# Scores of the second attention from two float32r parts stacked on the partitions, with the residual kept in DRAM meanwhile

## The chip, the cores and the metric

One NeuronCore of a Trainium2 chip runs the whole program. The metric is device microseconds from start to end of one launch; the time of the kernel before is the median of three runs. Engine names: PE is TensorE, PEld its weight loads, DVE is VectorE, ACT is ScalarE, POOL is GpSimd, SP the engine whose queue issues the DMAs.

## The reference, cut to what matters

The reference is two transformer blocks on x of 256 tokens by 1024 channels, in float32. The first block (indexed attention, pooling branch, a feed-forward layer of 16384 experts) is not touched by the change. The second block begins with a normalised projection to many parts: a recurrent branch (1344 channels), 16 query heads of 64, keys and values of 4 groups in three kinds (compressed, selected, window), gates, and two branch gates. Its attention, for each query head r of group g, is

```python
qh = rms_norm_2(heads(q, 16), q_norm_g)
k_cmp = rms_norm_2(compress(kc), ...); k_slc = rms_norm_2(ks, ...); k_win = rms_norm_2(kw, ...)
o_cmp = softmax(mask_cmp(qh @ k_cmp.T * scale)) @ v_cmp     # 15 compressed keys
o_slc = softmax(causal(qh @ k_slc.T * scale)) @ v_slc       # 256 keys
o_win = softmax(causal(qh @ k_win.T * scale)) @ v_win       # 256 keys
o = g0 * o_cmp + g1 * o_slc + g2 * o_win
```

With 256 tokens every block of keys is selected and the window covers them all, so the selected and the window kind are two plain causal softmaxes over different keys. After it x = x + (gated sum of the branches) @ w_out, then a feed-forward layer with its own residual x = x + ... .

## The kernel before, in words

Activations lie with channels on the partitions (x is [128, 8, 256]: 8 chunks of 128 channels, 256 tokens). Weights come as units of 512 KB: SP loads one into a raw buffer (`load`, L100), ScalarE copies it to a float32r tile `wh` (L164), VectorE or GpSimd subtracts to get the remainder `wl` (L165). `weights` (L169) hands the units out in a fixed order and keeps some ready ahead. `mm3` (L181) multiplies a unit with an activation that is split in the same way, in three float32r products: high by high, high by low, low by high; 24 matmuls of 256 columns for one unit.

The order in which each engine executes is laid down when the kernel is built. It follows the program's text with other work drawn forward where the dependencies allow it: a memset of the keys' tile (L956) stands between updates of x (L888), and transposes of one attention step stand between the scores of another. Each engine executes its own queue in order, except that weight loads can run ahead of matmuls.

The second block, in the program's order:

- L887 to L899: x is updated for the last time in the first block (L888, one VectorE operation per chunk), split by `make_xg` (L264), multiplied with the first three weight units; `sum_sq` and `rms_finish` give the token scale `r3` (reciprocal at L262).
- `proj` (L918) makes one projection of 128 channels into PSUM. Eleven go to the recurrent branch (L1026 to L1030), four to the inputs of the compression (L1035 to L1062; its tile `cb` shares the tag `P`), one to the gates, four to the values.
- `recur` (L1066) is the scan of the recurrent branch, advanced in pieces between projections.
- The keys, L1119 to L1133: for two kinds and two chunks c, the projection is scaled (`zs`, L930), squared, summed over each 64 channels by a float32 matmul with `blk64` (`hs` at L940, in `head_scale`), and VectorE writes the normalised keys (L1126). One chunk holds two groups, one on partitions 0 to 63 and one on 64 to 127. ScalarE copies each half to the other half as well (L1129), because a head's query lies on one half of the partitions. `ks` holds 15 compressed keys, one zero column and 256 selected keys, `kw` 256 window keys. The compressed keys are added at L1147.
- The queries, L1136 to L1156: eight projections, one ScalarE copy each with the norm's weight (L1154). One query chunk holds two heads, on 64 partitions each. Their norms are collected by `head_sq` and enter as a scale of the exponential.
- `nsa` (L1181) is a generator: for each group g and each block b of 128 queries there are five steps: scores of two heads and their exponentials, scores of the other two, then normalisation (L1247 to L1253) and the transposes of the compressed part, then twice transposes and products with the values. In block 0 two heads share one score tile; in block 1 each head has one of two PSUM banks. There are two score tiles. Scores are float32 matmuls with 64 rows (L1194, L1196, L1220, L1226), each in two records of the profile; masks are added by bf16 products of an identity with `mk0` and `mk1` (L1199, L1222, L1224, L1228). VectorE takes maxima (L1201, L1204, L1230, L1231), ScalarE makes exponentials with sums.
- L1313 to L1323: 26 more projections (recurrent gate and branch gates), with one or two steps of `nsa` after each. Then `wup2` (19 blocks for each of 8 output chunks), `wout2`, whose result is added to x (L1375), the feed-forward layer, and the last addition to x with the store of the output (L1411, L1412).

x stays in its tile in SBUF from the start to the end.

Of the kernel before, what the change touches and what calls it, by code (L numbers as in the profile page):

```python
# [7 lines left out]
F32 = mybir.dt.float32  # L8
# [50 lines left out]
def tile_kernel(ctx: ExitStack, tc: tile.TileContext, I, out):  # L59
    nc = tc.nc  # L60
# [14 lines left out]
    x = const.tile([128, 8, 256], F32, name="x")  # L75
# [8 lines left out]

    ones = const.tile([128, 128], F32, name="ones")
# [162 lines left out]
    def sum_sq(wpool_, tot, k, eng):  # L248
# [15 lines left out]
    def make_xg(dst, k, g):  # L264
# [640 lines left out]
    with ExitStack() as ph:  # L905
# [44 lines left out]
        def keys_of(t, g, s):  # L950

            return t[64 * s:64 * s + 64, 2 * (g % 2 != s) + g // 2]
# [3 lines left out]
        V.memset(ks[:, :, 15:16], 0.0)  # L956
# [78 lines left out]
        for kv in range(2):  # L1035
# [10 lines left out]
            cb = nw.tile([128, 16, 61], F32, name="cb", tag="P")  # L1046
# [72 lines left out]
        for dst, off, gn in ((ks, 16, "ksn"), (kw, 0, "kwn")):  # L1119
            for c in range(2):  # L1120
                z = scaled(proj())
                sq = squares(z)

                def key(dst=dst, off=off, gn=gn, c=c, z=z, sq=sq):
                    r = head_scale(sq)
                    V.scalar_tensor_tensor(dst[:, c, off:off + 256], z, vcol(gn), r, op0=OP.mult,  # L1126
                                           op1=OP.mult)
                    for d in (0, 64):
                        S.activation(dst[d:d + 64, 2 + c, off:off + 256],  # L1129
                                     dst[64 - d:128 - d, c, off:off + 256], AF.Copy)  # L1130

                late(key)
                next(rc, None)  # L1133
        q = ns.tile([128, 8, 256], F32, name="q2")
        ms = pxq.tile([128, 2, 16], F32, name="ms", tag="x")
        for c in range(8):  # L1136
            if c == 5:
# [5 lines left out]
                pk4, r4 = [t.rearrange("p (c s k) -> p s c k", c=2, s=2) for t in (pk, r[:, :60])]  # L1143
                for d in range(2):
                    for n in range(2):
                        rows = slice(64 * d, 64 * d + 64)
                        V.scalar_tensor_tensor(ks[rows, 2 * n:2 * n + 2, 0:15], pk4[rows, n ^ d],  # L1147
                                               vcol("kcn")[rows], r4[rows, n ^ d], op0=OP.mult, op1=OP.mult)
# [5 lines left out]
            S.activation(q[:, c], ps, AF.Copy, scale=vcol("qn"))  # L1154
# [26 lines left out]
        def nsa():  # L1181
            for g in range(4):
                for b in range(2):
                    n = 128 * (b + 1)
                    qs = slice(b * 128, (b + 1) * 128)
                    P = nw.tile([128, 4, 528], F32, name="P")
                    mx = nw.tile([128, 3, 4, 3], F32, name="nmx")
                    rg4 = rs[:, b, 4 * g:4 * g + 4]
                    for hp in range(2):
                        if b == 0:  # L1190
                            sc = pscore.tile([128, 2, 512], F32, name="sc")
                            for s in range(2):
                                qa = q[64 * s:64 * s + 64, 2 * g + hp, qs]
# [4 lines left out]
                                tc.add_manual_dep(m2.ins, m1.ins.name, no_sync(), reason="bank start")  # L1198
                                T.matmul(sc[:, s, 0:272], identb, mk0, start=False, stop=True,  # L1199
                                         skip_group_check=True)  # L1200
# [14 lines left out]
                        else:  # L1215
                            scs = []
                            for s in range(2):
                                sc = pscore.tile([128, 2, 512], F32, name="sc")
                                qa = q[64 * s:64 * s + 64, 2 * g + hp, qs]
                                T.matmul(sc[:, 0, 0:272], qa, keys_of(ks, g, s),  # L1220
                                         start=True, stop=False, skip_group_check=True)
                                T.matmul(sc[:, 0, 0:16], identb, mk1, start=False, stop=False,  # L1222
                                         skip_group_check=True)
# [11 lines left out]
                                scs.append([sc[:, 0, 0:16], sc[:, 0, 16:272], sc[:, 1, 16:272]])  # L1235
                        for s in range(2):
                            r = 2 * hp + s
                            for i, (o, w) in enumerate(((0, 16), (16, n), (16 + n, n))):
                                fact(P[:, r, o:o + w], scs[s][i], AF.Exp,
# [110 lines left out]
        sst.close()  # L1350
        pm4 = pool(ctx, "pm4", 4, side="right", space=PSUM)
# [19 lines left out]
        for m in range(8):  # L1371
# [3 lines left out]
            V.tensor_tensor(x[:, m], ps, x[:, m], OP.add)  # L1375
            late(lambda m=m: sum_sq(b2w, r4, m, G))
            make_xg(hf_, m, vcol("n2", m))
# [6 lines left out]
    with ExitStack() as ph:  # L1384
# [21 lines left out]
        for m in range(8):  # L1406
# [4 lines left out]
            V.tensor_tensor(x[:, m], ps, x[:, m], OP.add)  # L1411
            nc.sync.dma_start(out[:, m], x[:, m])  # L1412
# [112 lines left out]
```

## Time and profile before

| | |
|---|---|
| median of 3 runs | 1613.43 us (1612.01 to 1619.10) |
| the profiled execution | 1618.32 us, span 1616.6 us |
| busy: PE, DVE, ACT, POOL | 1565.8, 1267.8, 827.3, 210.7 us |
| granted TensorE clock over the span | 0.986 |
| DMA | 281.09 MB, 174 GB/s in the mean |

A stretch is named by microseconds from the span's start. A PE that is 100% busy can still wait a little, since the ends of pipelined matmuls are modelled; where the time of one matmul is wanted, the start of one is taken from the start of the next.

### The profile page before, as it was taken

Reading aid. Unit: us, or ns where it says so; the run is one execution under the profiler, and the core shown is the slowest. Engines: PE = TensorE matmul, PEld = TensorE weight load, DVE = VectorE, ACT = ScalarE, POOL = GpSimd, SP = SyncE. Lnnn points to the kernel's source line nnn. Section 1 sums busy time; section 2 is a strip of 40 time slices with the busy share of each in tenths; the row PEclk is TensorE's granted clock in tenths of the full one; section 3 lists DMA queues with packets and bytes.
Section 4 is the critical chain, followed back from the end, with each engine's and each line's share of the span. In section 5 each row is a group of like instructions: output and inputs, shape, how many; then the busy total and the mean of one; then the engine's idle time right before and its main releaser. Section 6 shows DMA issues by size and latency. Waiting matters only on the chain. (4 is left out here: it accounts for less than half of the span.)

```text
span 1616.6 us, 32864 instructions
## 1 busy us (share of the span) xinstructions
PE 1565.8 (97%) x13326; PEld 1509.9 (93%) x13326; DVE 1267.8 (78%) x2405; ACT 827.3 (51%) x1434; POOL 210.7 (13%) x156
## 2 busy tenths in 40 slices
PE   4999998999999999999999999998999999999999
PEld 3989998999999999999999999988977889999999
DVE  8789899984788887999856566979666666799963
ACT  3455563445444445443444444656656564576642
POOL 0100136795000000000000000035000000111100
PEclk9899999999999999999999999989999999999999
DMA  8668443555545545544566667453422224555553
GB/s 316 230 219 302 167 148 133 208 174 190 162 165 169 166 165 180 171 159 168 170 208 210 212 209 225 153 170 105 145 91 79 92 88 152 179 183 185 186 200 121
DMA packets 77927, 281.09 MB, mean 174 GB/s; under 512 B 8648, under 2 KB 9936, under 8 KB 77776
## 3 DMA queue, kind: packets, MB, share of 16 engines
q1 hardware_dynamic: 77776, 279.00, 51.6%
q8 instruction: 104, 1.70, 0.4%
q14 instruction: 47, 0.39, 0.1%
HBM read 277.92 MB, written 1.05 MB: 173 GB/s over the span
## 5 line engine op out<-in xcount | busy, mean ns | idle before, releaser
L164 ACT ACTIVATE wh<-raw 128x1024 fp32r<-128x1024 f32 x409 | 432.5, 1059 | 474.6 <-PE mm L188 244.8
L165 DVE TENSOR_TENSOR wl<-raw,wh 128x1024 fp32r<-128x1024 f32 x359 | 450.8, 1257 | 109.4 <-ACT wh L164 108.9
L852 PE MATMUL vo<-prh,spare 128*128 128x256 f32 x1024 | 181.1, 281 | 0.0
L852 PEld LDWEIGHTS vo<-prh,spare 128*128 128x128 f32 x1024 | 158.1, 190 | 0.0
L188 PE MATMUL mm<-h2h,wl 128*128 128x256 f32 x1024 | 143.6, 283 | 5.5 <-DVE wl L165 5.5
L188 PE MATMUL mm<-h2h,wh 128*128 128x256 f32 x1024 | 147.0, 286 | 0.0
L852 PE MATMUL vo<-prh,wh 128*128 128x256 f32 x512 | 146.7, 288 | 0.2 <-ACT prh L847 0.2
L188 PE MATMUL mm<-h2l,wh 128*128 128x256 f32 x1024 | 144.8, 285 | 0.0
L852 PE MATMUL vo<-prl,wh 128*128 128x256 f32 x512 | 144.5, 283 | 0.1
L254 POOL TENSOR_TENSOR r<-r,sq 128x256 f32<-128x256 f32 x18 | 14.5, 804 | 996.6 <-ACT sq L253 996.6
L852 PE MATMUL vo<-prh,wl 128*128 128x256 f32 x512 | 144.3, 283 | 0.0
L852 PE MATMUL vo<-prl,spare 128*128 128x256 f32 x512 | 143.9, 281 | 0.0
L165 POOL TENSOR_TENSOR wl<-raw,wh 128x1024 fp32r<-128x1024 f32 x50 | 134.2, 2701 | 68.6 <-ACT wh L164 41.6
L188 PEld LDWEIGHTS mm<-h2h,wl 128*128 128x128 f32 x1024 | 132.1, 192 | 5.9 <-DVE wl L165 5.9
L188 PEld LDWEIGHTS mm<-h2l,wh 128*128 128x128 f32 x1024 | 133.1, 193 | 0.0
L188 PEld LDWEIGHTS mm<-h2h,wh 128*128 128x128 f32 x1024 | 131.8, 192 | 0.2
L165 DVE TENSOR_TENSOR spare<-raw,spare 128x1024 fp32r<-128x1024 f32 x64 | 78.4, 1225 | 62.8 <-ACT spare L164 62.7
L164 ACT ACTIVATE spare<-raw 128x1024 fp32r<-128x1024 f32 x64 | 67.8, 1059 | 92.2 <-PE vo L852 89.5
L852 PEld LDWEIGHTS vo<-prl,wh 128*128 128x128 f32 x512 | 98.0, 191 | 0.2 <-DVE prl L848 0.2
L852 PEld LDWEIGHTS vo<-prh,wh 128*128 128x128 f32 x512 | 97.8, 191 | 0.3 <-ACT prh L847 0.3
L852 PEld LDWEIGHTS vo<-prh,wl 128*128 128x128 f32 x512 | 97.8, 191 | 0.2 <-DVE wl L165 0.2
L852 PEld LDWEIGHTS vo<-prl,spare 128*128 128x128 f32 x512 | 96.1, 188 | 0.0
(412 smaller groups left out, 3262.2 us busy)
## 6 DMA issues: line engine op xcount, KB each, us to landing
raw<-in_u_dram SPq DMA_DIRECT2D x128, 512.0 KB, 3.5
raw<-in_v_dram SPq DMA_DIRECT2D x128, 512.0 KB, 3.7
raw<-in_w_dram SPq DMA_DIRECT2D x86, 512.0 KB, 4.0
raw<-in_wada_dram SPq DMA_DIRECT2D x48, 512.0 KB, 5.0
raw<-in_wff_dram SPq DMA_DIRECT2D x48, 512.0 KB, 4.2
raw<-in_wup_dram SPq DMA_DIRECT2D x27, 512.0 KB, 4.1
raw<-in_wdn_dram SPq DMA_DIRECT2D x24, 512.0 KB, 3.5
raw<-in_wout_dram SPq DMA_DIRECT2D x16, 512.0 KB, 4.1
```

Of the source, the lines that this page charges most:

```text
L164: S.activation(u.h, t, AF.Copy)
L165: (G if n in on_pool and on_pool[n](i) else V).tensor_tensor(u.l, t, u.h.bitcast(F32), OP.subtract)
L188: T.matmul(ps, (u.l if wl else u.h)[:, s], a[al][:, k], start=start and n == 0, stop=stop and n == len(seq) - 1)
L254: eng.tensor_tensor(tot, tot, sq, OP.add)
L852: mm = T.matmul(vo[d // 2][:, d % 2], (u.l if wl else u.h)[:, d], pr[al][:, i % 2], start=(i == 0 and n == 0 and d % 2 == 0), stop=(i == 1 ...
```

## The change

The scores become float32r products over all 128 partitions. For one head, `q` holds the high part of the 64 query channels on the partitions where the projection left them and the low part on the other 64; `kh` holds the high part of the keys on both halves, `kl` the low part on both. The product with `kh` and the product with `kl` are added in PSUM, so that all four partial products of high and low are there. Keys of the two kinds lie in one tile of 528 columns for each group: 15 compressed, a zero, then by block of 128 keys selected and window. In block 1 the two banks therefore hold the first and the second block of keys, each of both kinds; the mask of the second bank covers 256 columns, and maxima and exponentials read the kinds across the banks. `q` doubles to 16 KB per partition. `kl` takes the place of x in SBUF: x is stored to DRAM before, and after the attention it is loaded into a new tile `x2`, which the rest of the kernel uses. The softmax's tile P gets one tag per block with one buffer each, and two small tiles (`rt`, `hrr`) one buffer.

```diff
-    x = const.tile([128, 8, 256], F32, name="x")
+    x = const.tile([128, 8, 256], F32, name="x", tag="x")
+    x_out = spill.tile([128, 8, 256], F32, name="x_out")
...
-            rt = b2w.tile([128, 256], F32, name="hrt")
+            rt = b2w.tile([128, 256], F32, name="rt", bufs=1)
...
-            r = b2w.tile([128, 256], F32, name="hrr")
+            r = b2w.tile([128, 256], F32, name="hrr", bufs=1)
...
-        ks = ns.tile([128, 4, 272], F32, name="ks")
-        kw = ns.tile([128, 4, 256], F32, name="kw")
+        kh = ns.tile([128, 4, 528], F32R, name="kh")
+        nc.sync.dma_start(x_out, x)
+        kl = const.tile([128, 4, 528], F32R, name="kl", tag="x")
...
-        V.memset(ks[:, :, 15:16], 0.0)
+        nought = ns.tile([128, 4, 1], F32, name="nought")
+        V.memset(nought, 0.0)
+        for t in (kh, kl):
+            V.tensor_copy(t[:, :, 15:16], nought)
...
-            cb = nw.tile([128, 16, 61], F32, name="cb", tag="P")
+            cb = nw.tile([128, 16, 61], F32, name="cb", tag=f"P{kv}", bufs=1)
...
                     r = head_scale(sq)
-                    V.scalar_tensor_tensor(dst[:, c, off:off + 256], z, vcol(gn), r, op0=OP.mult,
-                                           op1=OP.mult)
-                    for d in (0, 64):
-                        S.activation(dst[d:d + 64, 2 + c, off:off + 256],
-                                     dst[64 - d:128 - d, c, off:off + 256], AF.Copy)
+                    kt = b2w.tile([128, 256], F32, name="kt", tag="xt")
+                    V.scalar_tensor_tensor(kt, z, vcol(gn), r, op0=OP.mult, op1=OP.mult)
+                    for s in range(2):
+                        g = 2 * c + s
+                        src = kt[64 * s:64 * s + 64].rearrange("p (b k) -> p b k", b=2)
+                        for d in (s, 1 - s):
+                            h_, l_ = [t[64 * d:64 * d + 64, g, 16:528].rearrange(
+                                "p (b i k) -> p i b k", b=2, i=2)[:, kind] for t in (kh, kl)]
+                            S.activation(h_, src, AF.Copy)
+                            if d == s:
+                                own = h_
+                            V.tensor_tensor(l_, src, own.bitcast(F32), OP.subtract)
...
-        q = ns.tile([128, 8, 256], F32, name="q2")
+        q = ns.tile([128, 16, 256], F32R, name="q2")
...
-            S.activation(q[:, c], ps, AF.Copy, scale=vcol("qn"))
+            for s in range(2):
+                rows, other = slice(64 * s, 64 * s + 64), slice(64 - 64 * s, 128 - 64 * s)
+                S.activation(q[rows, 2 * c + s], ps[rows], AF.Copy, scale=vcol("qn")[rows])
+                V.scalar_tensor_tensor(q[other, 2 * c + s], ps[rows], vcol("qn")[rows],
+                                       q[rows, 2 * c + s].bitcast(F32), op0=OP.mult, op1=OP.subtract)
...
-                    P = nw.tile([128, 4, 528], F32, name="P")
+                    P = nw.tile([128, 4, 272 + 256 * b], F32, name="P", tag=f"P{b}", bufs=1)
...
-                                m1 = T.matmul(sc[:, s, 0:144], qa, keys_of(ks, g, s)[:, 0:144],
-                                              start=True, stop=False, skip_group_check=True)
-                                m2 = T.matmul(sc[:, s, 144:272], qa, keys_of(kw, g, s)[:, 0:128],
-                                              start=False, stop=False, skip_group_check=True)
+                                qa = q[:, 4 * g + 2 * hp + s, qs]
+                                T.matmul(sc[:, s, 0:272], qa, kh[:, g, 0:272], start=True, stop=False)
+                                T.matmul(sc[:, s, 0:272], qa, kl[:, g, 0:272], start=False, stop=False)
...
-                                T.matmul(sc[:, 0, 0:272], qa, keys_of(ks, g, s),
-                                         start=True, stop=False, skip_group_check=True)
-                                T.matmul(sc[:, 0, 144:272], identb, mk0[:, 16:144], start=False,
-                                         stop=True, skip_group_check=True)
-                                T.matmul(sc[:, 1, 16:272], qa, keys_of(kw, g, s),
-                                         start=True, stop=False, skip_group_check=True)
-                                T.matmul(sc[:, 1, 144:272], identb, mk0[:, 16:144], start=False,
-                                         stop=True, skip_group_check=True)
-                                V.tensor_reduce(mx[:, 0, 2 * hp + s, 1:3], sc[:, :, 16:272], AX, OP.max)
+                                T.matmul(sc[:, 0, 0:272], qa, kh[:, g, 0:272], start=True, stop=False)
+                                T.matmul(sc[:, 0, 0:272], qa, kl[:, g, 0:272], start=False, stop=False)
+                                T.matmul(sc[:, 0, 0:16], identb, mk1, start=False, stop=True)
+                                T.matmul(sc[:, 1, 16:272], qa, kh[:, g, 272:528], start=True, stop=False)
+                                T.matmul(sc[:, 1, 16:272], qa, kl[:, g, 272:528], start=False, stop=False)
+                                T.matmul(sc[:, 1, 16:272], identb, mk0[:, 16:272], start=False, stop=True)
+                                V.tensor_reduce(mx[:, 0, 2 * hp + s, 1:3], sc[:, :, 16:272].rearrange(
+                                    "p b (i k) -> p i b k", i=2), mybir.AxisListType.XY, OP.max)
...
         sst.close()
+        x2 = pool(ctx, "x2", side="right").tile([128, 8, 256], F32, name="x2")
+        nc.sync.dma_start(x2, x_out)
...
-            V.tensor_tensor(x[:, m], ps, x[:, m], OP.add)
+            V.tensor_tensor(x2[:, m], ps, x2[:, m], OP.add)
```

`sum_sq` and `make_xg` take x as an argument; after the attention they get `x2`. The compressed keys are made once over 128 rows and split by one ScalarE copy and one subtraction, in place of four VectorE operations of 64 rows.

## Rows read from the trace of the kernel before

**Rows 1.** The page, busy time of each engine, share of the span, instructions.
```profile
PE 1565.8 (97%) x13326; PEld 1509.9 (93%) x13326; DVE 1267.8 (78%) x2405; ACT 827.3 (51%) x1434; POOL 210.7 (13%) x156
```

**Rows 2.** Windows: length, busy (instructions) of PE PEld DVE ACT POOL, clock, DMA share, GB/s.
```profile
1120.00:1139.00 19.00, 18.39 (x127) 18.03 (x128) 18.86 (x23) 13.23 (x26) 0.89 (x1) 0.84 0.34 114
1139.00:1161.00 22.00, 22.00 (x192) 21.80 (x191) 10.23 (x18) 11.64 (x24) 0.00 (x0) 1.00 0.53 169
1161.00:1320.00 159.00, 158.70 (x1120) 128.14 (x1119) 100.28 (x229) 99.40 (x289) 0.00 (x0) 1.00 0.26 86
1320.00:1344.00 24.00, 24.00 (x178) 21.78 (x178) 14.69 (x28) 12.02 (x26) 0.00 (x0) 0.93 0.22 71
1344.00:1380.00 36.00, 36.00 (x304) 36.00 (x303) 22.99 (x36) 15.40 (x19) 0.00 (x0) 1.00 0.60 193
```

**Rows 3.** Waits, 1161 to 1320: who waited for whom, total, times, longest.
```profile
PEld pct L1256 <- DVE P L1253: 0.7, 2, 0.4
```

**Rows 4.** Timeline of PE, block 0: start, us, engine, line, operation.
```profile
1161.60 0.51 PE L1194 MATMUL sc<-ks,q 64*128 64x144 f32 x2
...
1162.26 0.29 PE L1199 MATMUL sc<-mk,identb 128*128 128x272 bf16 x1
1162.48 0.51 PE L1194 MATMUL sc<-ks,q 64*128 64x144 f32 x2
...
1163.14 0.29 PE L1199 MATMUL sc<-mk,identb 128*128 128x272 bf16 x1
1163.18 0.37 PE L188 MATMUL mm<-hbh,wh 128*128 128x256 f32 x1
```

**Rows 5.** Timeline of PE, block 1.
```profile
1173.69 0.72 PE L1220 MATMUL sc<-ks,q 64*128 64x272 f32 x2
1174.35 0.18 PE L1222 MATMUL sc<-mk,identb 128*128 128x16 bf16 x1
...
1175.16 0.23 PE L1228 MATMUL sc<-mk,identb 128*128 128x128 bf16 x1
1175.32 0.49 PE L1220 MATMUL sc<-ks,q 64*128 64x272 f32 x1
```

**Rows 6.** Groups by line and shape, 1120 to 1420: count, busy, mean ns.
```profile
L1220 PE MATMUL sc<-ks,q 64*128 64x272 f32 x32 | 11.6, 441 | 0.0
...
L1230 DVE TENSOR_REDUCE nmx<-sc 128x2 f32<-128x512 f32 x16 | 11.0, 691 | 9.6 <-PE sc L1228 9.5
...
L1194 PE MATMUL sc<-ks,q 64*128 64x144 f32 x32 | 8.1, 335 | 0.0
```

**Rows 7.** Line 991, a subtraction of this size: ns min/median/max.
```profile
L991 DVE TENSOR_TENSOR xl<-xt,xc x11: 409/415/953, 1025.3 to 1055.4; 128x256 fp32r<-128x256 f32 x10, 64x256 fp32r<-64x256 f32 x1
```

**Rows 8.** Timeline of DVE, the key chunks.
```profile
1127.65 0.48 DVE L1126 SCALAR_TENSOR_TENSOR ks<-zs,vec,hrr 128x256 f32<-128x256 f32 x1
1128.05 0.42 DVE L930 TENSOR_TENSOR zs<-mm,r 128x256 f32<-128x256 f32 x1
1128.39 1.74 DVE L944 RECIPROCAL hrr<-hrt 128x256 f32<-128x256 f32 x1
```

**Rows 9.** Timeline of PE, the same stretch.
```profile
1129.73 0.59 PE L940 MATMUL hs<-sq,blk 128*128 128x256 f32 x2
...
1132.99 0.69 PE L940 MATMUL hs<-sq,blk 128*128 128x256 f32 x2
```

**Rows 10.** Timeline of DVE, after the last update of x.
```profile
1011.78 0.47 DVE L888 SCALAR_TENSOR_TENSOR x<-vo,ada,x 128x256 f32<-128x256 f32 x1
...
1015.73 2.36 DVE L165 TENSOR_TENSOR wl<-raw,wh 128x1024 fp32r<-128x1024 f32 x2 [1.88 <-ACT wh L164]
1018.01 1.75 DVE L262 RECIPROCAL r<-rt 128x256 f32<-128x256 f32 x1
```

**Rows 11.** DMA issues, 1004 to 1013: KB each, median us to landing.
```profile
cw<-in_cw_dram SPq DMA_DIRECT2D x2, 512.0 KB, 6.0
```

**Rows 12.** Timeline of SP.
```profile
1016.98 10.96 SPq L102 DMA_DIRECT2D raw<-in_w_dram  x5
```

More of the change, by code (lines that the diff above doesn't have):

```diff
@@ L83, in vcol @@
         return vec[:, o:o + n]
+    spill = ctx.enter_context(tc.tile_pool(name="spill", bufs=1, space=bass.MemoryType.DRAM))
+    x_out = spill.tile([128, 8, 256], F32, name="x_out")
     ones = const.tile([128, 128], F32, name="ones")
@@ L246, in sqrt_next, with sum_sq @@
         fact(root, eps, AF.Sqrt)
-    def sum_sq(wpool_, tot, k, eng):
+    def sum_sq(wpool_, tot, k, eng, x=x):
         if k == 0:
@@ L262, in rms_finish, with make_xg @@
         V.reciprocal(r, rt)
-    def make_xg(dst, k, g):
+    def make_xg(dst, k, g, x=x):
         S.activation(dst[0][:, k, 0:256], x[:, k], AF.Copy, scale=g)
@@ L1117, in tile_kernel @@
                 next(rc)
-        for dst, off, gn in ((ks, 16, "ksn"), (kw, 0, "kwn")):
+        for kind, gn in enumerate(("ksn", "kwn")):
             for c in range(2):
@@ L1122, in tile_kernel, with key @@
                 sq = squares(z)
-                def key(dst=dst, off=off, gn=gn, c=c, z=z, sq=sq):
+                def key(kind=kind, gn=gn, c=c, z=z, sq=sq):
                     r = head_scale(sq)
-                    V.scalar_tensor_tensor(dst[:, c, off:off + 256], z, vcol(gn), r, op0=OP.mult,
-                                           op1=OP.mult)
-                    for d in (0, 64):
-                        S.activation(dst[d:d + 64, 2 + c, off:off + 256],
-                                     dst[64 - d:128 - d, c, off:off + 256], AF.Copy)
+                    kt = b2w.tile([128, 256], F32, name="kt", tag="xt")
[10 more added lines that the diff above has]
+                            V.tensor_tensor(l_, src, own.bitcast(F32), OP.subtract)
                 late(key)
                 next(rc, None)
-        q = ns.tile([128, 8, 256], F32, name="q2")
+        q = ns.tile([128, 16, 256], F32R, name="q2")
         ms = pxq.tile([128, 2, 16], F32, name="ms", tag="x")
@@ L1142, in tile_kernel @@
                 r = head_scale(squares(pk, 60), 60)
[L1143 to L1148, printed above, removed]
+                kt = nw.tile([128, 60], F32, name="ktc")
+                V.scalar_tensor_tensor(kt, pk, vcol("kcn"), r[:, :60], op0=OP.mult, op1=OP.mult)
+                kt = kt.rearrange("p (g k) -> p g k", g=4)
+                S.activation(kh[:, :, 0:15], kt, AF.Copy)
+                V.tensor_tensor(kl[:, :, 0:15], kt, kh[:, :, 0:15].bitcast(F32), OP.subtract)
                 pvc = px.tile([16, 4, 64], F32, name="pvc", tag="x")
@@ L1192, in nsa @@
                             for s in range(2):
-                                qa = q[64 * s:64 * s + 64, 2 * g + hp, qs]
-                                m1 = T.matmul(sc[:, s, 0:144], qa, keys_of(ks, g, s)[:, 0:144],
-                                              start=True, stop=False, skip_group_check=True)
-                                m2 = T.matmul(sc[:, s, 144:272], qa, keys_of(kw, g, s)[:, 0:128],
-                                              start=False, stop=False, skip_group_check=True)
-                                tc.add_manual_dep(m2.ins, m1.ins.name, no_sync(), reason="bank start")
-                                T.matmul(sc[:, s, 0:272], identb, mk0, start=False, stop=True,
-                                         skip_group_check=True)
+                                qa = q[:, 4 * g + 2 * hp + s, qs]
+                                T.matmul(sc[:, s, 0:272], qa, kh[:, g, 0:272], start=True, stop=False)
+                                T.matmul(sc[:, s, 0:272], qa, kl[:, g, 0:272], start=False, stop=False)
+                                T.matmul(sc[:, s, 0:272], identb, mk0, start=False, stop=True)
                             V.tensor_reduce(mx[:, 0, 2 * hp:2 * hp + 2, 1:3],
@@ L1238, in nsa @@
                             for i, (o, w) in enumerate(((0, 16), (16, n), (16 + n, n))):
-                                fact(P[:, r, o:o + w], scs[s][i], AF.Exp,
+                                dst = P[:, r, o:o + w]
+                                if b and i:
+                                    dst = dst.rearrange("p (b k) -> p b k", b=2)
+                                fact(dst, scs[s][i], AF.Exp,
                                              bias=mx[:, 1, r, i:i + 1], scale=rg4[:, r:r + 1],
@@ L1374, in tile_kernel @@
             mm3(ps, [(u, k, mix, k) for k in range(8)], by_block=m == 0)
-            V.tensor_tensor(x[:, m], ps, x[:, m], OP.add)
-            late(lambda m=m: sum_sq(b2w, r4, m, G))
-            make_xg(hf_, m, vcol("n2", m))
+            V.tensor_tensor(x2[:, m], ps, x2[:, m], OP.add)
+            late(lambda m=m: sum_sq(b2w, r4, m, G, x2))
+            make_xg(hf_, m, vcol("n2", m), x2)
         late()
@@ L1410, in tile_kernel @@
                 mm3(ps, [(u, k, ff, 8 * j + k) for k in range(8)], start=(j == 0), stop=(j == 2))
-            V.tensor_tensor(x[:, m], ps, x[:, m], OP.add)
-            nc.sync.dma_start(out[:, m], x[:, m])
+            V.tensor_tensor(x2[:, m], ps, x2[:, m], OP.add)
+            nc.sync.dma_start(out[:, m], x2[:, m])
 def prep(inputs):
```

8 lines of the change are left out of this document (2 added, 6 removed).

## The prediction, made before the changed kernel ran

> **What bounds it now.** I read the page first: TensorE is busy 97% of the span [rows 1]. Because that share averages stages with different limits, I then cut the second block into stages [rows 2]. What to see there: from 1161 to 1320 us, the stretch in which the attention steps are interleaved with the last 26 projections, TensorE is busy 158.7 of 159 us at full clock, while VectorE has 100.3 and ScalarE 99.4. From 1120 to 1139, where the keys are made, it is VectorE that is full (18.86 of 19 us) and the granted clock averages 0.84; from 1139 to 1161 TensorE is full again and VectorE under half busy. The waits come third [rows 3]: in the attention stage TensorE waits 0.7 us for the VectorE multiply behind the softmax, in two pieces. So in that stage a microsecond taken from TensorE comes off the end, as long as the softmax keeps up; ahead of 1139 a microsecond put on VectorE may go onto it.
>
> **The scores, taken away.** A pair of heads of block 0 runs from 1161.60 to 1163.18, 1.58 us, for four float32 products of keys and two mask products; the second mask costs 0.04 us, 1163.14 to 1163.18, because a float32r matmul follows [rows 4]. One head of block 1 takes 1.63 us, from 1173.69 to 1175.32, when another float32 head follows, and its last mask takes 0.16 of that [rows 5]. Each float32 product is two matmul records, so 32 records are 16 heads of either block [rows 6]: 8 pairs and 16 heads. Of each two heads of block 1 the second comes before something else; where that is a float32r matmul, 0.12 falls away, which I take for 8 of the 16: 8 x 1.58 + 16 x 1.63 - 8 x 0.12 = 37.8 us.
>
> **The scores, put in.** A float32r product of 256 columns costs 36.00 / 304 = 0.118 us in the stretch from 1344, which holds nothing else [rows 2]. A pair of block 0 becomes four such products (the parts of the keys, 272 columns) and two masks, 6 x 0.118 = 0.71; a head of block 1 four products, a mask of 256 columns, and one of 16 columns, which I take at the 0.04 of a mask ahead of float32r [rows 4]: 0.63. 8 x 0.71 + 16 x 0.63 = 15.8 us. Saved: 22.0. If the small mask costs a whole 0.118 the saving is 20.7. From 1320, just after the last float32 scores and with TensorE busy throughout, the clock averages 0.93 over 24 us [rows 2]: 3.4 us at half speed, which cost 1.7. They could vanish with those scores; I take 0 and keep 1.7 for the low end.
> Here a rule can be set against the rows. The Trainium skill (FP8 and Floating Point Precision, section TensorE Precision Notes) says that true FP32 makes four passes through the array. By passes alone the change would take away two of four: an estimate of 16 x 2 x (272 + 528) columns / 2.4 GHz = 10.7 us instead of 22.0. The trace differs: 272 columns hold TensorE from 1173.69 to 1174.35, 0.66 us [rows 5], where four passes would be 0.45.
>
> **What the shorter stage loses again.** The stage falls to about 137 us, and VectorE and ScalarE rise from 63% to 73% of it [rows 2]. There are 16 score steps (4 groups x 2 blocks x 2); in each the exponentials follow a reduction of 0.69 us [rows 6], and the score banks come free only after them. Bounds: 0, as the multiply is waited for 0.7 us in all today [rows 3]; 11 if every step waits for one reduction. Nearer to the small row, I take 4.
>
> **The keys.** Each of four key chunks now needs, on VectorE, four subtractions of 64 x 256 beside the product it had, and four ScalarE copies for two (ScalarE is off the path there, 13.2 of 19 us [rows 2]). The nearest subtraction row lasts 0.415 us for 128 x 256 [rows 7]; queued, an operation of this size holds VectorE 0.34 (zs starts at 1128.05, the next at 1128.39 [rows 8]). 16 x 0.34 = 5.4 us, in the stretch where VectorE is full. What is late next: a later chunk's scaled projection (zs), its square, and the head-norm matmul (hs), which stands ahead of a whole projection on TensorE. One hs has 0.59 us and the next 0.69 [rows 9], so the second already waits 0.1. The first chunk's subtractions (1.36 us) then push the third chunk's hs, and the second's push the fourth's: 2 x 1.36 less what other queued work can fill in. Bounds 0 and 5.4; I take 2.2.
>
> **The queries.** Eight times, a 128-row copy becomes two 64-row ScalarE copies and two VectorE operations, each of these at most 0.48, as the keys' product [rows 8]: 7.7 us more on VectorE and 3.8 on ScalarE in 1139 to 1161, where they have 10.2 and 11.6 of 22 us [rows 2]. Hidden, 0; without that cover up to 2.
>
> **The residual in DRAM.** The store of 1 MB can start when the last chunk of x is done, 1011.78 + 0.47 = 1012.25 [rows 10]. Two loads of 512 KB issued together land after 6.0 us [rows 11]; so it lands between 1018 and 1024 (the same bytes in the same time, or twice that). On SP little queues behind it: the next load goes out at 1016.98 [rows 12]. On VectorE the one-column copy into kl has to wait for the landing, and behind it stands whatever the queue has after it: the weight splits from 1015.73, the reciprocal at 1018.01, for which every projection's scaling waits [rows 10]. Bounds: 0 if the copy is queued after them, 8.6 (1015.7 to 1024.3) if ahead. VectorE idles 1.88 us there anyway; I take 1.5, and 0.5 for the zeros and the two one-column copies. The load back (1 MB) is wanted only after 8 x 19 blocks of three matmuls, 456 x 0.118 = 54 us, while DMA is at 0.22 to 0.60 [rows 2]: 0; uncovered it would be 6 to 12. On SP it waits for the last score that reads kh, behind loads already issued. P's two tags with one buffer each alternate as two buffers did: 0; so do the single rt and hrr, each read before the next is written.
>
> **Sum.** -22.0 + 4 + 2.2 + 2.0 = -13.8 us. The profiled execution took 1618.3 (its span of 1616.6 and 1.8 around it), 4.9 above the median of 1613.4; -13.8 gives 1604.5 against its own time and 1599.6 against the median, which I forecast as 1600, with 1590 to 1605 as this case's own range.
>
> **Rivals.**
> - *Half the saving.* Float32r weights cannot be loaded behind the masks and short products, and each of these takes the 0.22 us of a mask ahead of a float32 product, 1162.26 to 1162.48 [rows 4]. A pair is then 1.32 and a head 1.14: 37.8 - 28.8 = 9 us go, 1613.4 - 9 + 8.2 = 1613, no change. For it: that row; against: 0.118 where float32r stands alone. 12%. By the four passes of the Trainium skill, named above, the estimate would be 1611.
> - *VectorE takes it back.* The kl copy stands ahead of the splits (8.6) and all 5.4 of the keys reach the end: 1613.4 - 22 + 4 + 8.6 + 5.4 + 0.5 = 1610, no change. For it: VectorE is full before 1139; against: the 1.88 us of idle time, and a reciprocal that itself ends only at 1019.8 [rows 10], after the earlier landing. 9%.
> - *The clock.* In the attention stage TensorE begins to wait for the softmax, and the granted clock falls as in 1120 to 1139. At half clock work takes twice as long, so a part p of 137 us adds 137 p. Slower by 8 us needs 137 p = 13.8 + 8 = 21.8, p = 0.16, a mean clock of 1 / 1.16 = 0.86. At 0.84 (p = 0.19) it is 1613.4 - 13.8 + 26 = 1626. Against: the stage has 1.00 throughout today [rows 2]. 9%.
>
> **How the numbers follow.** The forecast has 70%. A measurement of this kernel tells about 0.5%, 8 us, from no change. Faster 0.70, same 0.12 + 0.09 = 0.21, slower 0.09. The range holds the forecast's case and the two unchanged ones: from all costs at 0 with the clock's gain (1613.4 - 23.7 = 1590) to the half saving, 1613.
>
> **What would show it.** A block-1 head near 0.63 us from its first score to the next head's, a pair near 0.71; the stage from first score to last transpose shorter by some 18 us, at clock 1.00; hs waiting 1 us or so at two of the chunks; the store landing by 1018 to 1024 with under 2 us of VectorE waiting for it; the load back waited for by nobody. Wrong: float32r scores above 0.2 us each, a clock below 0.9 in the stage, or TensorE idle above 10 us there.

## The result, and where the time went

The changed kernel takes 1597.46 us in the median of four runs (1595.31 to 1600.12), the kernel before 1613.87 in four runs beside it: a ratio of 0.9896, interval 0.9877 to 0.9916, 16.4 us less. The forecast was 1600, 13.8 us less. The profiled execution took 1595.43 us, its span 1593.0.

The page of the changed kernel, busy time of each engine as in [rows 1]:

```profile
PE 1539.8 (97%) x13278; PEld 1498.1 (94%) x13278; DVE 1278.1 (80%) x2437; ACT 834.4 (52%) x1451; POOL 211.3 (13%) x156
```

TensorE lost 26.0 us of busy time, and VectorE and ScalarE gained 10.3 and 7.1. The stages of [rows 2], shifted to where they now lie (windows, same columns):

```profile
1115.00:1132.00 17.00, 15.02 (x95) 14.28 (x96) 16.71 (x25) 10.98 (x21) 0.88 (x1) 0.83 0.26 93
1132.00:1165.00 33.00, 32.20 (x263) 30.74 (x262) 29.22 (x50) 23.80 (x46) 0.00 (x0) 1.00 0.50 160
1165.00:1306.00 141.00, 140.29 (x1097) 123.89 (x1096) 101.83 (x241) 102.31 (x305) 0.00 (x0) 1.00 0.30 96
1306.00:1330.00 24.00, 23.99 (x192) 22.03 (x191) 14.18 (x22) 10.05 (x14) 0.00 (x0) 1.00 0.49 166
```

In the attention stage TensorE is still busy 140.3 of 141 us at full clock, and the half clock behind it (0.93 in [rows 2]) has gone. Ahead of it, 1132 to 1165, VectorE went from under half to 29.2 of 33 us.

To place the gain I cut both executions at marks that both have: the first matmul on the second block's normalised input (`hbh`), the first head-norm sum of the keys (`hs`), the first and the last score record. Times in us; in brackets the projection matmuls that lie in the stretch.

The end is taken from the page's span, which is rounded to 0.1 us.

| stretch | before | after | difference |
|---|---|---|---|
| start to first `hbh` matmul | 1004.49 | 998.11 | -6.4 |
| to the first key sum `hs` | 116.12 | 117.57 | +1.5 |
| to the first score | 40.99 (264) | 49.81 (304) | +8.8 |
| first to last score | 158.82 (600) | 132.21 (560) | -26.6 |
| last score to the end | 296.18 | 295.30 | -0.9 |

The first line is not the change's: up to there TensorE executes the same 8662 matmuls in both. What differs is the clock, above all around 67 us; near 37 and near 283 us the kernel before has 3.41 us more at half speed as well. Windows of 60 to 80 us, the kernel before and then the changed one:

```profile
60.00:80.00 20.00, 20.00 (x117) 16.65 (x117) 15.67 (x47) 9.55 (x23) 4.00 (x9) 0.74 0.47 154
```
```profile
60.00:80.00 20.00, 20.00 (x152) 17.85 (x151) 19.22 (x68) 12.25 (x26) 7.09 (x17) 1.00 0.46 155
```

Where the granted clock averages 0.74, the 20 us hold 117 matmuls in place of 152. This half-speed piece, 10.24 us long, stands in the profiles of five of the changed kernel's variants below (`e1`, `e3`, `e6`, `e8`, `e9`) and of `e4`; in `e10` it is 6.83 us long, and the others have none there. So differences of a few us are read below from the first key sum to the end: 495.99 us before, 477.32 after. Two pieces of 3.41 us at half speed, worth up to 1.7 us each, also stand on opposite sides: one at 1001 us in the profile after, which goes with the +1.5, and one at 1320 us in the profile before, which goes with the -0.9. The run `e4_spill_alone` below keeps the old scores, lacks the piece at 1320, and has 294.77 us behind the last score: so that piece cost 1.4, and the changed kernel's 295.30 hides a loss of 0.5 behind the last score, whose place was not traced.

Between the first sum and the last score 40 projection matmuls changed sides: they are drawn ahead of the first score, at 0.12 us each 4.8 us. Net of them the way to the first score lost 4.0 us, and the attention stage won 21.8.

The timeline of PE in the changed kernel, two heads of block 0 (as [rows 4]):

```profile
1165.78 0.37 PE L1209 MATMUL sc<-kh,q 128*128 128x272 f32 x1
1166.00 0.29 PE L1210 MATMUL sc<-kl,q 128*128 128x272 f32 x1
1166.12 0.29 PE L1211 MATMUL sc<-mk,identb 128*128 128x272 bf16 x1
1166.16 0.37 PE L1209 MATMUL sc<-kh,q 128*128 128x272 f32 x1
1166.38 0.29 PE L1210 MATMUL sc<-kl,q 128*128 128x272 f32 x1
1166.51 0.29 PE L1211 MATMUL sc<-mk,identb 128*128 128x272 bf16 x1
1166.54 0.37 PE L1209 MATMUL sc<-kh,q 128*128 128x272 f32 x1
```

and one head of block 1 (as [rows 5]):

```profile
1171.55 0.39 PE L1231 MATMUL sc<-kh,q 128*128 128x272 f32 x1
1171.78 0.28 PE L1232 MATMUL sc<-kl,q 128*128 128x272 f32 x1
1171.91 0.18 PE L1233 MATMUL sc<-mk,identb 128*128 128x16 bf16 x1
1171.95 0.36 PE L1234 MATMUL sc<-kh,q 128*128 128x256 f32 x1
1172.15 0.28 PE L1235 MATMUL sc<-kl,q 128*128 128x256 f32 x1
1172.27 0.28 PE L1236 MATMUL sc<-mk,identb 128*128 128x256 bf16 x1
1172.31 0.60 PE L190 MATMUL mm<-hbh,wh 128*128 128x256 f32 x3
```

A pair that nothing cuts into takes 0.76 us (1165.78 to 1166.54) where it took 1.58, a head also 0.76 where it took 1.63. In both, a mask's own start to the next start is 0.04, and the product behind it takes 0.20 to 0.23 where its neighbours take 0.12 to 0.13. Summed from start to start, all scores fell from 37.97 to 18.62 us: 19.35. The other 2.4 of the stage's 21.8 lie in the matmuls around them: a projection matmul there takes 0.127 us in the mean where it took 0.129, and the transposes of P gave 0.75 in all; why was not traced.

### The profile page after: what moved, and what is told of

The parts are those of the page before. It is cut to its first block, busy times and chain, and to the rows that moved or that the text cites. A ratio compares the mean times of both kernels' runs of the same rounds, so it can differ in the third digit from the quotient of the medians.

```text
span 1593.0 us, 32813 instructions
## 1 busy us (share of the span) xinstructions
PE 1539.8 (97%) x13278; PEld 1498.1 (94%) x13278; DVE 1278.1 (80%) x2437; ACT 834.4 (52%) x1451; POOL 211.3 (13%) x156
## 4 chain that ended last, share of the span: by engine, by line
PE 74%; DVE 6%; ACT 1%; issue 1%; DMA 0%; POOL 0%; ACTq 0%; POOLq 0%; DVEq 0%
PE mm L190 43%; PE vo L854 22%; PE gt L797 2%; DVE wl L167 2%; PE npo L1295 2%; PE pgt L1022 1%; PE npo L1298 1%; PE phd L1062 1%; DVE ri L1088 1%; PE npt L1286 0%; ACT wh L166 0%; DVE ri L1078 0%; DVE xt L992 0%; DVE hrr L946 0%; DVE eq L721 0%
```

## The experiments

Every kernel ran in the same way beside the kernel before, four to six times (`e4_spill_alone` twelve times), and one execution of each was profiled. All marks in one table, first the two kernels of the prediction. Columns: from the first key sum to the third; to the fourth, with projection matmuls between; to the first score, likewise; first to last score; first key sum to the end; median of the runs.

| kernel | 3rd sum | 4th sum | first score | scores | to the end | median |
|---|---|---|---|---|---|---|
| before | 9.12 | 12.38 (72) | 40.99 (264) | 158.82 | 495.99 | 1613.87 |
| after | 9.77 | 15.33 (83) | 49.81 (304) | 132.21 | 477.32 | 1597.46 |
| r0_after | 9.78 | 15.33 (83) | 49.86 (304) | 132.22 | 477.44 | 1595.54 |
| e1_one_product | 9.76 | 15.32 (83) | 49.86 (304) | 126.80 | 471.42 | 1594.34 |
| e6_masks_last | 9.77 | 15.32 (83) | 49.85 (304) | 130.58 | 475.71 | 1593.86 |
| e3_square_first | 9.77 | 15.33 (83) | 44.63 (276) | 135.34 | 475.36 | 1595.75 |
| e4_spill_alone | 8.97 | 12.36 (72) | 40.98 (264) | 158.83 | 494.54 | 1614.05 |
| e2_keys_pool | 9.78 | 13.78 (72) | 50.64 (304) | 132.23 | 478.28 | 1600.49 |
| e7_square_masks | 9.77 | 15.33 (83) | 46.13 (276) | 133.95 | 475.48 | 1592.44 |
| e8_all_three | 9.78 | 13.78 (72) | 44.98 (283) | 132.98 | 473.34 | 1594.72 |
| e9_far_copies_pool | 9.04 | 15.65 (83) | 50.49 (304) | 132.23 | 478.09 | 1599.20 |
| e10_far_and_subs_pool | 9.22 | 12.86 (72) | 49.98 (304) | 132.25 | 477.67 | 1594.69 |
| e11_best | 8.96 | 15.63 (83) | 44.93 (276) | 133.95 | 474.34 | 1592.60 |
| e12_all_four | 8.96 | 12.85 (72) | 44.75 (283) | 132.96 | 472.97 | 1591.22 |

**The yardstick**, the changed kernel unaltered.

> The changed kernel once more, as the yardstick for the other three of this call: 0.990 of the kernel before, 16 us less. If the time really went where the two traces put it, the stretch from the first to the last score is again 132 us, and the stretch from the first use of the projection weights to the last of them 89 us.

It came out at 0.9872 (0.9853 to 0.9892), and first to last score is 132.22 us again; the stretch of the projection weights is not among the marks. From the first sum to the end the two profiles differ by 0.12 us, so differences of half a us there are read from one profile each, where the half-speed pieces are the same. Two profiles differ in these behind the first sum: `e7` has one more, as said below, and `e3` has 3.41 us less of it, but its third and fourth sums come at the same times.

**Is TensorE still the bound of the stage?**

```diff
-T.matmul(sc[:, s, 0:272], qa, kl[:, g, 0:272], start=False, stop=False)
...
-T.matmul(sc[:, 0, 0:272], qa, kl[:, g, 0:272], start=False, stop=False)
...
-T.matmul(sc[:, 1, 16:272], qa, kl[:, g, 272:528], start=False, stop=False)
```

> Leaves out the low part of the keys: the 48 products of the queries with kl are not made, all else stays. Theory (TensorE still sets the pace of the attention stage): 16 of 272 columns in block 0, 16 of 272 and 16 of 256 in block 1, at 0.12 to 0.125 us from one start to the next, so 5.9 us less than the changed kernel, and a stage of 126 us from first to last score. Rival (the softmax on VectorE and ScalarE has become the bound): less than 1.5 us, with TensorE waiting for the exponentials or the multiply behind the softmax instead.

From the first sum to the end 6.0 us went (477.44 to 471.42), 5.4 of them between the scores. Its stage, by windows:

```profile
1170.00:1297.00 127.00, 126.57 (x983) 110.62 (x981) 93.59 (x221) 94.62 (x285) 0.00 (x0) 1.00 0.30 98
```

TensorE is still busy 126.6 and VectorE 93.6 of 127 us. So the softmax had not become the bound: the 4 us that I took for it were not lost.

**Where do the scores cost more than forecast?**

```diff
 T.matmul(sc[:, 0, 0:272], qa, kl[:, g, 0:272], start=False, stop=False)
-T.matmul(sc[:, 0, 0:16], identb, mk1, start=False, stop=True)
 T.matmul(sc[:, 1, 16:272], qa, kh[:, g, 272:528], start=True, stop=False)
 T.matmul(sc[:, 1, 16:272], qa, kl[:, g, 272:528], start=False, stop=False)
+T.matmul(sc[:, 0, 0:16], identb, mk1, start=False, stop=True)
 T.matmul(sc[:, 1, 16:272], identb, mk0[:, 16:272], start=False, stop=True)
```

This is block 1; in block 0 the two masks move into a loop of their own behind the four products. The kernel before has the mask of 16 columns directly ahead of another mask too (L1222 and L1224).

> Only the order of TensorE's score matmuls changes: in block 0 both masks stand behind the four products, in block 1 the mask of 16 columns stands directly ahead of the one of 256. Theory (a mask of 16 columns is too short to cover the weight load of the product behind it; a mask of 256 or 272 columns covers it): a head of block 1 falls from 0.76 to 0.64 us, 16 x 0.12 = 1.9 us in all, and a pair of block 0 stays at 0.76. Rival (each step from a bf16 mask to a float32r product costs 0.1 us, whatever the length): heads fall as well, and pairs fall too, from 0.76 to 0.66, 2.7 us in all. Third (no order matters): 0.

The timeline of PE with the masks last, one head of block 1:

```profile
1175.80 0.39 PE L1232 MATMUL sc<-kh,q 128*128 128x272 f32 x1
1176.03 0.29 PE L1233 MATMUL sc<-kl,q 128*128 128x272 f32 x1
1176.15 0.28 PE L1234 MATMUL sc<-kh,q 128*128 128x256 f32 x1
1176.27 0.28 PE L1235 MATMUL sc<-kl,q 128*128 128x256 f32 x1
1176.39 0.18 PE L1236 MATMUL sc<-mk,identb 128*128 128x16 bf16 x1
1176.42 0.27 PE L1237 MATMUL sc<-mk,identb 128*128 128x256 bf16 x1
1176.45 0.36 PE L190 MATMUL mm<-hbh,wh 128*128 128x256 f32 x1
```

A head falls from 0.76 to 0.65 us, and the stage by 1.64 (132.22 to 130.58); 16 x 0.11 would be 1.8. A pair of block 0 goes from 0.76 to 0.74 (1170.40 to 1171.14, from a `kh` product behind masks to the next matmul behind masks), not to 0.66:

```profile
1170.40 0.38 PE L1209 MATMUL sc<-kh,q 128*128 128x272 f32 x1
...
1170.99 0.41 PE L1212 MATMUL sc<-mk,identb 128*128 128x272 bf16 x2
1171.14 1.20 PE L190 MATMUL mm<-hbh,wl 128*128 128x256 f32 x8
```

So a mask of 272 columns costs what a product of that width costs, 0.125, though its 0.04 hides it: the rest is in the product behind. A mask of 16 columns costs nearly as much, unless another mask stands behind it. That pairs fell by 0.02 alone rules out a price on every step from a mask to a float32r product. A weight load left uncovered fits all of this: the load for the product behind the small mask starts at 1171.91, with the mask, and lasts to 1172.11; the product behind that one starts at 1172.15. The lines of the weight loads of the changed kernel:

```profile
1171.91 0.10 PEld L1233 LDWEIGHTS <-identb 128*128 128x128 bf16 x1
1171.91 0.20 PEld L1234 LDWEIGHTS sc<-kh,q 128*128 128x128 f32 x1
```

The record of this load lasts 0.20 us, and the next load starts 0.12 behind it (1172.03). The Trainium skill (TensorE: Matmul & The Clock Gate, section LDWEIGHTS) gives a load as its columns over 1.2 GHz, for 128 columns an estimate of 0.107 us; the 0.11 that a head gave back and the 0.12 between loads agree with it, the record's 0.20 does not.

**What delays the first score: the queries.**

```diff
 ps = proj()
+sq = squares(ps)
 for s in range(2):
 ...
-late(lambda sq=squares(ps), c=c: head_sq(ms, c, sq))
+late(lambda sq=sq, c=c: head_sq(ms, c, sq))
```

> In the loop over the queries the square on ScalarE is issued ahead of the four operations that split the queries. Theory (the square stands behind operations of both engines that read the same PSUM tile one after another, and the sum over heads made from it holds up TensorE in the middle of the projections): the waits of those sums for the square fall from 0.4 us and more to under 0.1, and the time by 1 to 2.4 us. Rival (the extra time there is only VectorE's, full with the splits, or the drawn-forward projections): no gain, within 0.5 us, and the sums of the queries wait for something else.

Waits of TensorE's weight loads in the query stretch, the changed kernel (its profile `r0_after`, 1131 to 1166) and then this one (1137 to 1167):

```profile
PEld ms L226 <- ACT sq L937: 1.4, 5, 0.4
PEld hs L942 <- ACT sq L937: 1.0, 1, 1.0
PEld pr L1179 <- ACT vc L1163: 0.6, 1, 0.6
```
```profile
PEld hs L942 <- ACT sq L937: 1.0, 1, 1.0
PEld pr L1180 <- ACT vc L1163: 0.6, 1, 0.6
```

The waits of the sums for the square are gone, and 2.1 us with them (477.44 to 475.36). One thing that held the square is named among the waits of the changed kernel, 1131 to 1166:

```profile
ACT sq L937 <- DVE q L1168: 0.5, 2, 0.3
```

The square and the splits read one PSUM tile from two engines, one after another. These 0.5 us are less than the 1.4 that the sums waited: the square also stood behind ScalarE's own copies, one of which waits for a split itself (`r0_after`, 0.23 us at 1145.99). The run moves the square ahead of all four operations at once, so it shows that their order cost 2.1 us, not the share of each; the 0.7 beyond the 1.4 was not traced. The Trainium skill (PSUM — Partial Sum Buffer, section PSUM bank collisions raise a hardware error) says that the compiler orders any two accesses of different engines to one bank and quarter of the partitions; the wait of ScalarE for a VectorE read of the same tile agrees.

**Does the trip of the residual cost anything?**

```diff
+nc.sync.dma_start(x_out, x)
+kl = const.tile([128, 4, 528], F32R, name="kl", tag="x")
+V.tensor_copy(kl[:, :, 15:16], nought)
...
+nc.sync.dma_start(x2, x_out)
```

> The kernel before, float32 scores and all, with only the round trip of the residual: x is stored to DRAM at the same place, a tile takes its slot and gets the one-column copy, and x2 is loaded back after the last score. Theory (the copy is queued behind work that waits longer, and the load back is hidden): from the first projection matmul to the end within 0.5 us of the kernel before, 612.1 us. Rival, the terms of the prediction: 2.0 us more. Second rival (the copy holds up VectorE's queue until the store has landed): 3 to 8.6 us more.

0.9998 (0.9985 to 1.0011). From `hbh` to the first sum 116.25 us where the kernel before has 116.12, and from there 494.54 where it has 495.99; that difference is the half clock at 1320, absent here. The 116.25 is two differences that cancel. TensorE's first product with a low part comes 0.97 us later than before (3.40 us behind the first `hbh` matmul, 2.42 before), because memsets for the recurrent branch, ahead of a weight split in VectorE's queue, wait 0.91 us there; the store is issued only 7 us later, at 1012.30. By 38 us behind the first `hbh` TensorE is 1.6 us late, for a reason not traced, and it gets 1.5 of that back where the half-speed piece near 1065 lasts 6.83 us here and 10.24 before. So this run alone does not show that the trip is free; the changed kernel's own trace does. There the first product with a low part is 0.14 us late, the lag on the kernel before is 1.59 us where the half clock at 1001 ends, 1.69 behind the copy, and 1.42 at 70 us behind the first `hbh`. VectorE's timeline shows why:

```profile
1010.98 1.23 DVE L167 TENSOR_TENSOR wl<-raw,wh 128x1024 fp32r<-128x1024 f32 x1 [3.37 <-ACT wh L166]
1012.12 0.17 DVE L960 CAST kl<-nought 128x4 fp32r<-128x4 f32 x1
1012.19 1.22 DVE L167 TENSOR_TENSOR wl<-raw,wh 128x1024 fp32r<-128x1024 f32 x1
```

The store is issued at 1006.04 and landed after 3.9 us; the copy runs 2.2 us after that, behind a weight split that waits for ScalarE in any case. The load back, 6.8 us, is waited for by nobody. So the trip cost 0.24 us at most (0.14 and 0.10).

**What delays the first score: the keys.** First the subtractions alone.

```diff
-V.tensor_tensor(l_, src, own.bitcast(F32), OP.subtract)
+G.tensor_tensor(l_, src, own.bitcast(F32), OP.subtract)
```

> The sixteen subtractions that make the low part of the keys go from VectorE to GpSimd, which has nothing to do in the changed kernel from 1117 to 1166 us. Theory (these subtractions push the scaled projection, the square and the head-norm sum of the later key chunks): from the first to the fourth head-norm sum 15.3 us with 83 projection matmuls become about 13.7, so 1 to 1.7 us come back. Rival (the chunks wait for ScalarE or the half clock there, not for VectorE): 0, within 0.5. Second rival (GpSimd at 0.9 to 1.2 us for such an operation, 14 to 19 us in all, holds the buffer of the normalised keys longer than VectorE did): slower by 1 us or more.

Neither theory held in full. The fourth sum came 1.55 us earlier, but with 11 fewer matmuls (1.3 us) ahead of it, so net only by 0.2; the third stayed at 9.78, and to the end 0.8 us were lost. What holds the third sum is on ScalarE. Its timeline, the kernel before and then the changed one, second key chunk:

```profile
1127.06 0.47 ACT L197 ACTIVATE hrt<-hs,eps 128x256 f32<-128x256 f32 x1 [0.67 <-PE hs L940]
1128.17 0.84 ACT L1129 ACTIVATE ks<-ks 64x256 f32<-64x256 f32 x2 [0.63 <-DVE ks L1126]
1129.04 0.42 ACT L935 ACTIVATE sq<-zs 128x256 f32<-128x256 f32 x1
```
```profile
1122.40 0.47 ACT L199 ACTIVATE rt<-hs,eps 128x256 f32<-128x256 f32 x1 [0.93 <-DVE hrr L946]
1123.23 1.72 ACT L1138 ACTIVATE kh<-kt 64x256 fp32r<-64x256 f32 x4 [0.36 <-DVE kt L1131]
1124.98 0.42 ACT L937 ACTIVATE sq<-zs 128x256 f32<-128x256 f32 x1
```

The square of the next chunk stands behind the copies: 0.84 us of them before, 1.72 now. (The square root waits 0.93 us for the reciprocal that reads the single buffer `rt`, but the reciprocal behind it starts 7.8 us after the first sum in both kernels, so nothing came of that.) VectorE then holds the fourth chunk (changed kernel, timeline of DVE):

```profile
1125.11 1.66 DVE L1141 TENSOR_TENSOR kl<-kt,kh 64x256 fp32r<-64x256 f32 x4
1126.80 0.48 DVE L1131 SCALAR_TENSOR_TENSOR kt<-zs,vec,hrr 128x256 f32<-128x256 f32 x1
1127.20 1.22 DVE L167 TENSOR_TENSOR wl<-raw,wh 128x1024 fp32r<-128x1024 f32 x1
1128.34 1.71 DVE L1141 TENSOR_TENSOR kl<-kt,kh 64x256 fp32r<-64x256 f32 x4
1130.08 0.42 DVE L932 TENSOR_TENSOR zs<-mm,r 128x256 f32<-128x256 f32 x1
```

Its scaled projection `zs` starts 14.4 us after the first sum; before, 10.9. Two runs took these apart:

```diff
-S.activation(h_, src, AF.Copy)
 if d == s:
+    S.activation(h_, src, AF.Copy)
     own = h_
+else:
+    G.tensor_copy(h_, src)
```

> Of the four copies of the normalised keys for each chunk, the two to the other half of the partitions go from ScalarE to GpSimd; the subtractions stay on VectorE. Theory (two copies more on ScalarE, 0.86 us, hold the next chunk's square, and so its head-norm sum; VectorE's subtractions hold the fourth chunk besides): the third sum comes 9.1 us after the first, as before the change, instead of 9.8, the fourth is still late, and from the first sum to the end it is 476.7 us where the changed kernel has 477.4. Rival (ScalarE has nothing to do with it): the third sum stays at 9.8, and nothing is gained.

> These copies and all sixteen subtractions on GpSimd. Theory (ScalarE's two copies and VectorE's subtractions each delay the chain, so that taking one away alone gives little): from the first to the fourth sum 12.4 us with 72 projection matmuls, as before the change, where the subtractions alone on GpSimd gave 13.8 with 72. Rival: 13.8 again, or more, if GpSimd with six operations of 1 us for each chunk holds the buffer of the normalised keys.

With the far copies off ScalarE the third sum is back at 9.04, and with the subtractions off VectorE too the fourth comes at 12.86 with 72 matmuls, 0.5 from before. Both causes of the late key sums are shown. Yet neither run gains at the end: 478.09 (476.7 was expected) and 477.67 against 477.44. The second shows where it went; the waits of TensorE's weight loads, 1132 to 1170:

```profile
PEld ms L226 <- ACT sq L937: 3.2, 7, 1.1
PEld hs L942 <- ACT sq L937: 0.4, 1, 0.4
```

The waits of the query sums for their squares grew from 1.4 to 3.2 us.

**Together.** `e7` joins the diffs of `e3` and `e6`; `e8` adds that of `e2` to these, `e11` that of `e9`, and `e12` both.

> The changed kernel with both edits that TensorE gained from: the square issued first in the loop over the queries, and the masks last in each pair or head. They lie in different stretches, so theory: the gains add up, 2.1 + 1.6 = 3.7 us from the first projection matmul to the end, 595.3 - 3.7 = 591.6 us. Rival (work drawn ahead by the one takes the place that the other wins): 2 us.

> The same with the subtractions of the keys on GpSimd as well. If these subtractions cost 1.65 us on VectorE, 590.0 us from the first projection matmul to the end; if they are not what the key chunks wait for, 591.6; if GpSimd is too slow for them, 592.5 or more.

> The square first in the queries, the masks last in the scores, and the far copies of the keys on GpSimd. If the gains add up, 477.4 - 2.1 - 1.6 - 0.7 = 473.0 us from the first head-norm sum of the keys to the end; if the far copies give nothing, 473.7.

> The square first, the masks last, and both the far copies and the subtractions of the keys on GpSimd. Theory (the sums of the keys and the sums of the queries are one chain of small steps ahead of the first score: what the keys win is lost again where the next square waits, unless the query loop is freed too): with the square first, the 12.9 us from the first to the fourth sum now count, and from the first sum to the end it is 472.3 to 473.0 us, where the subtractions alone on GpSimd gave 473.3 and the far copies alone 474.3. Rival (the keys never cost anything at the end; only the queries did): 473.5 or more.

The square and the masks gave 475.48 to the end, with a piece of 3.41 us at half clock at 1144 that the others lack. It costs 1.5 by the first score (46.13, where `e3` has 44.63) and at most 1.7, which leaves 473.8 to 474.0 as an estimate: 3.4 to 3.6 of the expected 3.7. The subtractions on GpSimd besides (`e8`) gave 473.34, about 0.5 better, a third of the 1.65 in question. The far copies alone (`e11`) gave nothing, 474.34, and so missed both values expected. All four (`e12`) gave 472.97, 4.5 us less than the changed kernel: at the upper edge of what the chain theory said and clear of the rival's 473.5. So the keys do count once the queries are freed, though only for 0.8 to 1.0 us, read from one profile each. `e12` has the shortest time of this study, 1591.22 us, 0.9851 of the kernel before (0.9829 to 0.9872), an interval that overlaps those of `e7` and `e11`. Its way to the first score is still 44.75 - 40.99 - 19 x 0.12 = 1.5 us longer than before the change; what holds that stays open.

## Why the prediction was right, term by term

The forecast held in sign and mechanism: TensorE bounded the attention stage, what was taken from it came off the end, and the clock there stayed at 1.00. That 1600 lies so near the median is in part luck: the scores and the small steps ahead of them came out worse than forecast (by 2.7 and 1.8 us), the stage, the trip of the residual and the matmuls around the scores better (by 4, 2 and 2.4). The sizes:

- **Scores taken away**, forecast 37.8: measured 37.97.
- **Scores put in**, forecast 15.8: 18.62, so 19.35 saved where I had 22.0, and even my low bound of 20.7 was missed. The step that failed is the mask "at the 0.04 of a mask ahead of float32r". I read the 0.04 between two starts as the mask's cost; the rest of it is moved to the product behind, which that product's next start would have shown. From start to start the 16 heads of block 1 took 11.85 us where I had 10.1; with the masks side by side (`e6`) they took 10.25, so 1.6 hung on that mask. The 8 pairs of block 0 took 6.76 where I had 5.7: 272 columns take 0.125 and not 0.118, which makes 0.3, and the rest lies mostly where transposes and products with the values cut into a pair (eight uncut pairs would be 8 x 0.76 = 6.1).
- **The four passes of the Trainium skill**, which would have saved 10.7 us: the float32 products cost more than passes alone, as [rows 5] had said, and 19.35 went.
- **The stage loses again**, forecast 4: nothing. That the waits grow with the busy share of VectorE was a guess, and the run without the low products (`e1`) shows room for 6 us more.
- **Keys 2.2 and queries 0**: together 4.0 net. The keys' place was right (TensorE idles 0.59 and 0.71 us ahead of the third and fourth sums), their cause half: "ScalarE is off the path there" is the step that failed, since ScalarE's queue, busy for 13.2 of 19 us, held the square behind the copies. For the queries I asked whether VectorE and ScalarE had time, not what stands behind the splits: the square, and behind it the sums on TensorE. 2.1 us hung on that order.
- **Residual in DRAM**, forecast 2.0: 0.24 us at most. The store landed after 3.9 us, not 6 to 12, and the copy was queued where VectorE waits anyway. The load back cost nothing, as forecast.
- **The half clock at 1320**, forecast to stay: gone, for 0.9 us net (1.4 gained, 0.5 lost behind the last score). With the cheaper matmuls around the scores (2.4) it makes up for the shortfall of the scores.

From the first `hbh` to the end the profiles differ by 612.11 - 594.89 = 17.2 us: the terms give 19.35 + 2.4 - 4.0 + 0.9 - 1.5 = 17.2, the last being the half clock at 1001. Of the rivals, *half the saving* fell with 0.76 for pairs and heads (it wanted 1.32 and 1.14), *the clock* with 1.00 in the stage; *VectorE takes it back* had a true part, the key sums, and a false one, the splits behind the `kl` copy.

## What to carry to other kernels

Read a matmul's cost from the start of the one behind it to the next start too: behind a very short product the next one took 0.20 us in place of 0.12, so put short products together, ahead of a long one. When a change adds small operations to an engine with spare time, ask what stands behind them in its queue and who waits for that; a busy share of 70% said nothing here. Where two such queues feed one chain, freeing one may show no gain until the other is free as well.

## What the runs showed of the hardware

- A product of 16 columns between float32r products cost about 0.11 us more than the same one ahead of another mask.
- With the subtractions on GpSimd, a VectorE product of two SBUF tiles, 0.48 us by itself, took 0.96 two of the three times that it ran beside one, and 0.49 the third time; the two subtractions of 64 x 256 that it then met took 1.62 and 1.63 us, the ones behind them 0.82. Timeline of DVE with the subtractions on GpSimd:

```profile
1126.09 0.96 DVE L1131 SCALAR_TENSOR_TENSOR kt<-zs,vec,hrr 128x256 f32<-128x256 f32 x1
```

- The granted clock falls to half for 10.24 us near 67 us in some profiles and not in others, though TensorE's matmuls are the same up to there and it is busy for all of 60 to 80 us in both. Half of that, an estimate of 5.1 us, is a third of what this change is worth. What sets it off was not tried.
